# Second RMSNorm of a decoder layer: scaling the first block between the last residual additions

## The chip, the cores and the metric

One core of a Trainium2 chip runs the whole layer in one launch. The metric is device microseconds from the start to the end of one execution; the figure for a kernel is the median of three executions. PE is the matrix engine, PEld its weight loads, DVE the vector engine, ACT the scalar engine, POOL the GpSimd engine, SP the queue that issues the transfers.

## The reference, cut to what matters

Every tensor is float32. Only the lines around the second norm matter here; 1088 tokens (1024 of the prompt and 8 x 8 of the samples) with 1024 channels pass through them.

```python
x = x + jnp.concatenate([a, o], axis=-1) @ w_out           # output projection, residual
h = rms_norm(x, norm_ffn_g)                                # x * rsqrt(mean(x*x) + EPS) * g, per token
g_full = jnp.concatenate([ffn_past, h @ w_ffn_gate], axis=1)
g = depthwise_conv_valid(g_full, ffn_conv_w, ffn_conv_b)   # causal, width 3
x = x + (jax.nn.silu(g) * (h @ w_ffn_up)) @ w_ffn_down     # w_ffn_gate, w_ffn_up: 1024 x 2816
```

## The kernel before

Channels lie on the 128 partitions and tokens along the free axis, so x is eight tiles `x2[0..7]` of 128 x 1088. Each float32 product is made from two rounded parts per operand, `hi` and `lo`, as three matmuls: hi x hi, hi x lo and lo x hi. `split` (L907) makes them: ACT copies `hi` (L909), DVE subtracts to get `lo` (L910). The tokens fall into two halves of HN = 544 columns.

**Last part of the output projection.** `out_half(h, hook)` (L974) walks over the eight tiles m. For each it forms one product (`block_product`, 2 chunks x 2 k x 3 = 12 matmuls of 272 columns, L849 to L852) in one of four PSUM pairs; DVE adds it to x (L982), SP stores x to DRAM (L983), ACT squares it (L985), and from m = 1 on DVE adds the square to a running sum (L989). The half h = 0 comes first, then h = 1. A hook is called after each m of the second half.

**The norm.** `root` (L185) sums over the partitions with five matmuls against a column of ones, which run as ten (L192, in one PSUM pair), and makes the reciprocal root of each token on DVE and ACT (L196 to L207). `spread` (L210) turns that column back into a row on all partitions with five transposes on PE (L219) and two ACT copies (L221). Its result `rs[0]` serves the first half, `rs[1]` the second. `scale` (L993, L995) multiplies a tile by the norm's weight and that row, in place, on DVE.

**The first gate and up products.** `first_blocks(k, tag)` scales and splits four tiles of the first half. `first_half` (L1019) multiplies them with two weight blocks at once (`two_products`, L855): per tile k there are 12 matmuls, 6 into `px` and 6 into `py`. Four tiles are `b11`, the other four `b21`; between the two, ACT copies the partial results out of PSUM (L1026). The same products follow for the up weights (`up0`), and `second_half` for the other half of the tokens. The remaining ten pairs of blocks of the gated network (`ffn_pair`, L1111) run by a Strassen-like scheme of seven products, whose sums and differences of weights start with the addition at L952.

**What sets the order.** Each engine works through its own queue in order and stops at an instruction whose inputs are not there. The queues are laid out when the kernel is built, by a planner that goes by program order and by its own estimates of when things are ready. `tc.issue_after(ins)` pins the instructions traced inside it behind `ins` in the queue of the engine of `ins`; it adds no wait between engines. In the kernel before, the scales of the first block stand behind `added`, the last running sum of the second half, and so do the splits:

```python
def first_blocks(k, tag, after):
    for i in range(k, k + 4):
        with tc.issue_after(made[-2] if len(made) > 1 else after):
            scale(0, i, rs[0])
        with tc.issue_after(after):
            split(x2[i][:, :HN], tag, i - k)
```

`made` lists the DVE subtractions of the splits in the order in which they were traced; `made[7]` is that of the eighth tile.

Of the kernel before, what the change touches and what calls it, by code (L numbers as in the profile page):

```python
# [5 lines left out]

# [1 line left out]

# [54 lines left out]
HN = N // 2  # L65
HF = NF // 2
PO = 240
# [10 lines left out]
def trunk_kernel(tc, xT, w_in, w_out, w_gate, w_up, w_down, par, kc, vc, sa, sf, pmask, smask,  # L78
                 yT, kT, vT, ca, cas, cf):
    nc = tc.nc  # L80
    with (
# [34 lines left out]
        def zt(z, tag, bufs, s, w=N, dt=F32):  # L116
            return zone[z].tile([P, w], dt, tag=tag, name=nm(s), bufs=bufs)

        def keep(s, w=N):
            return tp.tile([P, GW], F32, tag="T", name=nm(s))[:, :w]  # L120
# [64 lines left out]
        def root(sq, div, width):  # L185


            ps = bank(*rbank[0])
            size = sizes(width)
            nt = len(size)  # L190
            for i, n in enumerate(size):
                nc.tensor.matmul(ps[:n, i:i + 1], sq[:, i * P:i * P + n], ones, start=True, stop=True)  # L192
            v = sp.tile([P, 9], F32, tag="rv", name=nm("rv"), bufs=2)[:, :nt]
            nc.vector.memset(v, 1.0)
            nf = width // P
            nc.vector.tensor_scalar(v[:, 0:nf], ps[:, 0:nf], 1.0 / div, EPS, op0=ALU.mult, op1=ALU.add)  # L196
            if nf < nt:
                n = size[-1]
                nc.vector.tensor_scalar(v[:n, nf:nt], ps[:n, nf:nt], 1.0 / div, EPS, op0=ALU.mult, op1=ALU.add)
            r = sp.tile([P, 9], F32, tag="rr", name=nm("rr"), bufs=2)[:, :nt]  # L200
            nc.vector.reciprocal(r, v)
            nc.scalar.activation(r, r, AF.Sqrt)

            t = sp.tile([P, 9], F32, tag="rt", name=nm("rt"), bufs=2)[:, :nt]
            nc.vector.tensor_mul(t, r, r)
            nc.vector.scalar_tensor_tensor(t, t, -0.5, v, op0=ALU.mult, op1=ALU.mult)
            nc.vector.scalar_tensor_tensor(r, t, 1.5, r, op0=ALU.add, op1=ALU.mult)  # L207
            return r
# [55 lines left out]
        with ExitStack() as order:  # L264
            for k in range(KT):
                t = keep("x")
# [488 lines left out]
        i = 0  # L755
        for p in range(NS1, NP):
            prompt_heads(i, HEADS[p - NS1])
            i = HEADS[p - NS1]
# [12 lines left out]
        x2 = []  # L771
# [42 lines left out]
        for p, upto in zip(range(NS1, NP), SHEADS):  # L814
            prompt_heads(i, upto)
            i = max(i, upto)
# [13 lines left out]
        def pair(s="g"):  # L830

            return zone["Fps"].tile([P, 1024], F32, tag="g2", name=nm(s), bufs=4)
# [4 lines left out]
        def slot(tag, s, dt=F32R, w=HN):  # L837
            return zt("F", tag, 8, s, HN, dt)[:, :w]

        def block_product(o, w, x, start):  # L840

            whi, wlo = w
            nk = len(x)
            for c in range(2):
                n = HN // 2
                ps = o[:, PO:512] if c == 0 else o[:, 512:PO + HN]
                for k, (xh, xl) in enumerate(x):
                    t = slice(c * n, c * n + n)
                    nc.tensor.matmul(ps, whi[:, k, :], xh[:, t], start=(start and k == 0), stop=False,  # L849
                                     skip_group_check=True)  # L850
                    nc.tensor.matmul(ps, whi[:, k, :], xl[:, t], start=False, stop=False, skip_group_check=True)  # L851
                    nc.tensor.matmul(ps, wlo[:, k, :], xh[:, t], start=False, stop=(k == nk - 1),  # L852
                                     skip_group_check=True)

        def two_products(outs, ws, x, start, hook=lambda k, last: None):  # L855


            n = HN // 2
            nk = len(x)
            for k, (xh, xl) in enumerate(x):  # L860
                for o, (whi, wlo) in zip(outs, ws):
                    for c in range(2):
                        ps = o[:, PO:512] if c == 0 else o[:, 512:PO + HN]
                        t = slice(c * n, c * n + n)
                        nc.tensor.matmul(ps, whi[:, k, :], xh[:, t], start=(start and k == 0), stop=False,
                                         skip_group_check=True)
                        nc.tensor.matmul(ps, whi[:, k, :], xl[:, t], start=False, stop=False, skip_group_check=True)
                        last = nc.tensor.matmul(ps, wlo[:, k, :], xh[:, t], start=False, stop=(k == nk - 1),
                                                skip_group_check=True).ins
                hook(k, last)  # L870

        def all_of(ps):
            return ps[:, PO:PO + HN]

        def halves(x):
            return x[:, :HN], x[:, HN:N]
# [3 lines left out]
        n = PARTS[-1]  # L880
# [24 lines left out]
        made = []  # L905

        def split(x, tag, k):  # L907
            hi, lo = slot(tag, tag + "h"), slot(tag, tag + "l")
            nc.scalar.activation(hi, x, AF.Copy)  # L909
            made.append(nc.vector.tensor_sub(lo, x, hi.bitcast(F32)).ins)  # L910
            blocks[tag][k] = hi, lo
# [6 lines left out]
        def weight_raw(w, j):  # L918
            raw = []
            for i in (j, j + HF):  # L920
                raw.append(wp.tile([P, D], F32, tag="WR", name=nm("wr"), bufs=WR))
                with tc.issue_after(last_load):
                    nc.sync.dma_start(raw[-1], w[i])
            return raw
# [9 lines left out]
        def block_tile(x, zone=False):  # L934

            t = zt("F", "WA", 2, "wa", D, F32R) if zone else wp.tile([P, D], F32R, tag="W", name=nm("wb"))
            hi, lo = t[:, :half], t[:, half:]
            nc.scalar.activation(hi, x, AF.Copy)  # L938
            nc.gpsimd.tensor_sub(lo, x, hi.bitcast(F32))  # L939
            return [t.rearrange("p (k c) -> p k c", c=P) for t in (hi, lo)]  # L940
# [4 lines left out]
        def weight_blocks(w, j):  # L945

            g, u = weight_raw(w, j)
            g1, g2, u1, u2 = g[:, :half], g[:, half:], u[:, :half], u[:, half:]
            a11 = block_tile(g1, True)
            a12 = block_tile(g2, True)  # L950
            x = zt("F", "tmp", 4, "s1", HN)[:, :half]
            nc.vector.tensor_add(x, u1, u2)  # L952
            nc.vector.tensor_sub(u1, g1, u1)
            nc.vector.tensor_sub(g1, x, g1)  # L954
            s2 = block_tile(g1)
            s1 = block_tile(x)
            nc.vector.tensor_sub(g2, g2, g1)
            s3 = block_tile(u1)
            s4 = block_tile(g2)
            a22 = block_tile(u2)  # L960
            return [a11, a12, a22, s1, s2, s3, s4]
# [12 lines left out]
        def out_half(h, hook):  # L974


            c = slice(h * HN, h * HN + HN)
            for m in range(KT):
                ps = pair()
                block_product(ps, wl[m], part[h], True)  # L980
                x = x2[m][:, c]
                added = nc.vector.tensor_add(x, all_of(ps), x).ins  # L982
                nc.sync.dma_start(x2d[m][:, c], x)  # L983
                s = slot("t1", "sq", F32)
                nc.scalar.activation(s, x, AF.Square)  # L985
                if m == 0:
                    acc = s
                else:
                    added = nc.vector.tensor_add(acc, s, acc).ins  # L989
                hook(m, added)  # L990
            return acc, added

        def scale(h, k, r):  # L993
            x = x2[k][:, h * HN:h * HN + HN]
            nc.vector.scalar_tensor_tensor(x, x, col(C_GFFN + k), r, op0=ALU.mult, op1=ALU.mult)  # L995

        def new_root(s):
            return slot("t3", s, F32)

        sq0, _ = out_half(0, lambda *_: None)  # L1000
        rs = []

        def norm_first(m, added):
            if m == 1:
                rs.append(root(sq0, D, HN))
            elif m == 4:
                rs[0] = spread(rs[0], new_root, HN)

        def first_blocks(k, tag, after):
            for i in range(k, k + 4):  # L1010
                with tc.issue_after(made[-2] if len(made) > 1 else after):
                    scale(0, i, rs[0])
                with tc.issue_after(after):
                    split(x2[i][:, :HN], tag, i - k)

        sq1, added = out_half(1, norm_first)
        quads = [(*halves(x2[k]), *halves(x2[k + 4])) for k in range(4)]

        def first_half(w, between=lambda: None, hook=lambda k, last: None):  # L1019
# [20 lines left out]

        def between():
            rs.append(root(sq1, D, HN))
            first_blocks(4, "b21", added)

        def spread_second(k, last):
            if k == 1:
                with tc.issue_after(last):
                    rs[1] = spread(rs[1], new_root, HN)

        first_blocks(0, "b11", added)  # L1050
        g1, g_shared = first_half(gate0, between, spread_second)
        r1 = rs[1]
        for k in range(4):
# [2 lines left out]
        u1, u_shared = first_half(up0)  # L1056
# [54 lines left out]
        def ffn_pair(j):  # L1111
# [58 lines left out]
            if j:  # L1170
                products(weight_blocks(w_up, j), u11, put_u)
                return
# [215 lines left out]
```

## Time and profile before

| | |
|---|---|
| median of three runs | 1409.12 us |
| the three runs | 1405.84 to 1413.22 us |
| the profiled execution, its own time | 1410.36 us |
| its span, first to last instruction | 1408.6 us |
| PE busy in the span | 1348.9 us, 96% |
| DVE, ACT, POOL busy | 844.7, 521.9, 447.0 us |
| mean granted PE clock | 0.982 |

The span is that of the profiled execution alone; 1.8 us of its own time lie outside it. The output projection's last part and the first blocks of the second norm lie between 600 and 657 us. A busy share is an average over the whole span, so it tells little of these 57 us; the rows below are taken from them.

### The profile page before, as it was taken

The numbers are of one execution on the slowest core, as the hardware profiler recorded it, in microseconds if no ns is written. First come the engines' busy times: TensorE is split into PE (matmuls) and PEld (weight loads), VectorE is DVE, ScalarE is ACT, GpSimd is POOL, SyncE is SP. The second block draws the span as 40 slices with busy tenths as digits, with TensorE's granted clock in tenths as the row PEclk, the third lists the DMA queues.
The fourth block names the chain that finished last, engine by engine and source line by source line (L and its number), as shares of the span: only waits on it lengthen the run. The fifth ranks groups of instructions, "written<-read, shape, count | busy, mean of one in ns | idle before, by whom it ended". The sixth has DMA issues, their size and how long they took to land.

```text
span 1408.6 us, 25028 instructions
## 1 busy us (share of the span) xinstructions
PE 1348.9 (96%) x10059; PEld 1282.0 (91%) x10059; DVE 844.7 (60%) x1636; ACT 521.9 (37%) x1047; POOL 447.0 (32%) x362
## 2 busy tenths in 40 slices
PE   6999999999998999988999999999999999999995
PEld 6988879899977777988999999999999999999995
DVE  7398595556674656677965555665655543322146
ACT  5312212456564564254533333333332332112033
POOL 3221111111001103330754654554654222233124
PEclk9999999999999999998999999999999999999998
DMA  7247676836798878450112222212222672313003
GB/s 275 57 140 248 222 256 206 224 111 168 197 266 229 256 213 257 128 195 24 47 50 89 93 77 77 92 47 77 92 78 77 202 275 60 117 57 123 12 16 113
DMA packets 84884, 195.17 MB, mean 139 GB/s; under 512 B 12576, under 2 KB 46752, under 8 KB 84768
## 3 DMA queue, kind: packets, MB, share of 16 engines
q1 hardware_dynamic: 84768, 193.57, 43.7%
q8 instruction: 79, 1.29, 0.4%
q14 instruction: 37, 0.30, 0.1%
HBM read 145.03 MB, written 48.52 MB: 137 GB/s over the span
## 4 chain that ended last, share of the span: by engine, by line
PE 76%; DVE 10%; issue 5%; DMA 5%; POOL 2%; ACT 1%; SPq 1%; POOLq 0%; DVEq 0%; ACTq 0%
PE g L174 10%; PE g L172 10%; PE g L173 10%; PE py L849 4%; PE py L851 4%; PE py L852 4%; DVE cacc L342 4%; PE o L675 3%; PE s L590 3%; PE pz L852 3%; PE pz L849 3%; PE pz L851 3%; PE px L849 3%; PE px L852 3%; PE px L851 3%
## 5 line engine op out<-in xcount | busy, mean ns | idle before, releaser
L148 POOL TENSOR_TENSOR wl<-wr,wh 128x768 fp32r<-128x768 f32 (+2 forms) x61 | 116.8, 1916 | 461.6 <-PE g L174 373.6
L172 PE MATMUL g<-xh,wh 128*128 128x384 f32 (+1 forms) x472 | 158.1, 335 | 0.0
L173 PE MATMUL g<-xl,wh 128*128 128x384 f32 (+1 forms) x472 | 156.6, 332 | 0.0
L174 PE MATMUL g<-xh,wl 128*128 128x384 f32 (+1 forms) x472 | 156.5, 332 | 0.0
L173 PE MATMUL g<-al,wh 128*128 128x384 f32 (+1 forms) x432 | 143.2, 332 | 1.7 <-DVE al L1203 1.7
L172 PE MATMUL g<-ah,wh 128*128 128x384 f32 (+1 forms) x432 | 141.6, 333 | 2.2 <-ACT ah L1202 0.8
L174 PE MATMUL g<-ah,wl 128*128 128x384 f32 (+1 forms) x432 | 142.7, 332 | 0.7 <-POOL wl L148 0.7
L146 ACT ACTIVATE wh<-wr 128x768 fp32r<-128x768 f32 (+2 forms) x62 | 52.0, 839 | 240.1 <-PE g L174 177.8
L939 POOL TENSOR_TENSOR wb<-wr,wb 128x512 fp32r<-128x512 f32 x84 | 115.2, 1383 | 56.8 <-ACT wb L938 56.8
L1225 DVE TENSOR_TENSOR x<-g,x 128x384 f32<-128x384 f32 (+1 forms) x72 | 38.0, 534 | 137.8 <-PE g L174 137.6
L938 ACT ACTIVATE wb<-wr 128x512 fp32r<-128x512 f32 x84 | 52.4, 628 | 164.2 <-DVE wr L954 105.0
L631 ACT ACTIVATE y<-y,m 128x128 f32<-128x128 f32 (+1 forms) x192 | 88.4, 463 | 32.2 <-DVE m L619 32.1
L1143 DVE SCALAR_TENSOR_TENSOR fc<-gb,prm,fc 128x1104 f32<-128x1104 f32 x44 | 83.5, 1918 | 14.7 <-ACT fc L1141 14.4
L174 PEld LDWEIGHTS g<-xh,wl 128*128 128x128 f32 x472 | 89.3, 189 | 2.6 <-issue 2.5
L172 PEld LDWEIGHTS g<-xh,wh 128*128 128x128 f32 x472 | 89.6, 190 | 1.4 <-issue 1.2
L173 PEld LDWEIGHTS g<-xl,wh 128*128 128x128 f32 x472 | 89.6, 190 | 1.1 <-issue 1.0
L594 DVE CUSTOM_DVE_ANT_0 y<-s,pmk 128x128 f32<-128x128 f32 (+1 forms) x192 | 63.9, 378 | 41.6 <-PE s L590 33.2
L939 POOL TENSOR_TENSOR wa<-wr,wa 128x512 fp32r<-128x512 f32 x42 | 54.9, 1308 | 101.0 <-ACT wa L938 101.0
L172 PEld LDWEIGHTS g<-ah,wh 128*128 128x128 f32 x432 | 81.7, 190 | 3.1 <-ACT ah L1202 1.1
L173 PEld LDWEIGHTS g<-al,wh 128*128 128x128 f32 x432 | 82.1, 190 | 2.4 <-DVE al L1203 2.4
L174 PEld LDWEIGHTS g<-ah,wl 128*128 128x128 f32 x432 | 82.1, 190 | 1.0 <-POOL wl L148 1.0
L342 DVE SCALAR_TENSOR_TENSOR cacc<-gp,prm,cacc 128x1024 f32<-128x1024 f32 x60 | 77.9, 1299 | 0.1
(358 smaller groups left out, 4133.0 us busy)
## 6 DMA issues: line engine op xcount, KB each, us to landing
cr<-in_kc SPq DMA_DIRECT2D x24, 768.0 KB, 8.4
cr<-in_vc SPq DMA_DIRECT2D x24, 768.0 KB, 7.1
kk<-dk SPq DMA_DIRECT2D x48, 256.0 KB, 7.5
u<-u SPq DMA_DIRECT2D x22, 544.0 KB, 3.2
ur<-u SPq DMA_DIRECT2D x22, 544.0 KB, 5.4
wr<-in_w_in SPq DMA_DIRECT2D x22, 512.0 KB, 5.2
wr<-in_w_gate SPq DMA_DIRECT2D x22, 512.0 KB, 3.3
wr<-in_w_up SPq DMA_DIRECT2D x22, 512.0 KB, 5.0
```

The lines of the kernel that those rows point to most:

```text
L148: lo_eng.tensor_sub(lo, raw, hi.bitcast(F32))
L172: nc.tensor.matmul(ps[c], whi[:, k, :], xh[:, t0:t0 + n], start=(k == 0), stop=False)
L173: nc.tensor.matmul(ps[c], whi[:, k, :], xl[:, t0:t0 + n], start=False, stop=False)
L174: nc.tensor.matmul(ps[c], wlo[:, k, :], xh[:, t0:t0 + n], start=False, stop=(k == nk - 1))
L342: eng.scalar_tensor_tensor(acc[:, :S], gp[:, j:j + S], col(w0 + j), acc[:, :S], op0=ALU.mult, op1=ALU.add)
L594: nc.vector.tensor_tensor_reduce(out=y[:, o:o + n], in0=ps[:, o:o + n], in1=mask, op0=ALU.add, op1=ALU.min, scale=1.0, scalar=3e38, accum_ ...
L631: nc.scalar.activation(y, y, AF.Exp, bias=m[:, 4 * g + i:4 * g + i + 1], scale=-1.0, accum_out=den[:, g, 2 * hd + u, i:i + 1])
L849: nc.tensor.matmul(ps, whi[:, k, :], xh[:, t], start=(start and k == 0), stop=False, skip_group_check=True)
L851: nc.tensor.matmul(ps, whi[:, k, :], xl[:, t], start=False, stop=False, skip_group_check=True)
L852: nc.tensor.matmul(ps, wlo[:, k, :], xh[:, t], start=False, stop=(k == nk - 1), skip_group_check=True)
L939: nc.gpsimd.tensor_sub(lo, x, hi.bitcast(F32))
L1143: nc.vector.scalar_tensor_tensor(c[:, :W], gb[i][:, t:t + W], col(C_FW + 3 * f + t), c[:, :W], op0=ALU.mult, op1=ALU.add)
```

## The change

The sums of squares keep their arithmetic, and so does everything else; only places and orders change.

1. `root` of the first half moves from m = 1 to m = 3 of the second half's loop, and its `spread` from m = 4 to m = 6.
2. `out_half` returns the list of residual additions. The first scale is pinned behind the addition of m = 6, the second behind that of m = 7; the others stay two splits behind. The splits are no longer pinned, so sums of squares may come later than scales.
3. In `two_products` the matmuls of tile k are pinned behind the last matmul of tile k-1 on PE, for all four calls of it.
4. The first addition of each later set of weight sums (L952) is pinned behind the eighth split of the first block.

```diff
@@ two_products
+            last = None
             for k, (xh, xl) in enumerate(x):
-                for o, (whi, wlo) in zip(outs, ws):
-                    for c in range(2):
+                with tc.issue_after(last) if last else nullcontext():
+                    for o, (whi, wlo) in zip(outs, ws):
+                        for c in range(2):
...
-                        last = nc.tensor.matmul(ps, wlo[:, k, :], xh[:, t], start=False, stop=(k == nk - 1),
-                                                skip_group_check=True).ins
+                            end = nc.tensor.matmul(ps, wlo[:, k, :], xh[:, t], start=False, stop=(k == nk - 1),
+                                                   skip_group_check=True).ins
+                last = end
                 hook(k, last)
@@ weight_blocks
-            nc.vector.tensor_add(x, u1, u2)
+            with tc.issue_after(made[7]):
+                nc.vector.tensor_add(x, u1, u2)
@@ out_half
+            residuals = []
...
-                added = nc.vector.tensor_add(x, all_of(ps), x).ins
+                residuals.append(nc.vector.tensor_add(x, all_of(ps), x).ins)
...
-                    added = nc.vector.tensor_add(acc, s, acc).ins
-                hook(m, added)
-            return acc, added
+                    nc.vector.tensor_add(acc, s, acc)
+                hook(m)
+            return acc, residuals
@@ norm_first
-            if m == 1:
+            if m == 3:
                 rs.append(root(sq0, D, HN))
-            elif m == 4:
+            elif m == 6:
                 rs[0] = spread(rs[0], new_root, HN)
@@ first_blocks
-                with tc.issue_after(made[-2] if len(made) > 1 else after):
+                with tc.issue_after(made[-2] if len(made) > 1 else residuals[6 + i]):
                     scale(0, i, rs[0])
-                with tc.issue_after(after):
-                    split(x2[i][:, :HN], tag, i - k)
+                split(x2[i][:, :HN], tag, i - k)
```

## Rows read from the trace of the kernel before

**Rows 1.** By stretch: us, busy PE PEld DVE ACT POOL, granted clock, DMA, GB/s.
```profile
618.80:622.40 3.60, 0.00 (x0) 0.02 (x1) 3.46 (x5) 2.47 (x5) 1.03 (x2) 1.00 0.57 190
623.30:626.60 3.30, 3.30 (x17) 3.27 (x17) 1.86 (x8) 0.91 (x2) 1.81 (x2) 0.52 0.47 168
...
635.10:638.80 3.70, 0.01 (x1) 0.01 (x1) 3.50 (x6) 1.34 (x3) 0.00 (x0) 0.77 0.40 151
637.50:647.30 9.80, 8.51 (x39) 8.48 (x40) 9.77 (x19) 4.87 (x9) 0.00 (x0) 0.50 0.01 3
...
656.80:1360.00 703.20, 697.73 (x5114) 695.73 (x5113) 373.89 (x461) 221.90 (x305) 301.12 (x261) 1.00 0.26 87
```

**Rows 2.** PE's longest waits from 600 to 700 us: in total, times, longest.
```profile
PE px L865 <- DVE x L995: 3.7, 1, 3.7
PE g L192 <- DVE sq L989: 3.7, 1, 3.7
```

**Rows 3.** Timeline of PE: start, duration, work, idle before and its releaser.
```profile
612.21 0.29 PE L849 MATMUL g<-mh,wh 128*128 128x272 f32 x1
...
613.71 0.29 PE L849 MATMUL g<-mh,wh 128*128 128x272 f32 x1
...
618.47 0.29 PE L852 MATMUL g<-mh,wl 128*128 128x272 f32 x1
622.41 1.20 PE L192 MATMUL g<-ones,sq 128*128 128x1 f32 x10 [3.65 <-DVE sq L989]
623.54 0.59 PE L849 MATMUL g<-mh,wh 128*128 128x272 f32 x1
...
624.38 0.43 PE L849 MATMUL g<-mh,wh 128*128 128x272 f32 x1
624.61 0.43 PE L851 MATMUL g<-ml,wh 128*128 128x272 f32 x1
...
629.60 0.77 PE L219 MATMUL g<-ident,rr 128*128 128x128 f32 x5
...
634.80 0.28 PE L852 MATMUL g<-mh,wl 128*128 128x272 f32 x1
638.79 0.60 PE L865 MATMUL px<-b11h,wa 128*128 128x272 f32 x1 [3.71 <-DVE x L995]
...
639.41 1.89 PE L192 MATMUL g<-ones,sq 128*128 128x1 f32 x10
641.23 0.59 PE L867 MATMUL px<-b11l,wa 128*128 128x272 f32 x1
...
656.84 0.29 PE L865 MATMUL px<-b11h,wa 128*128 128x272 f32 x1
```

**Rows 4.** Timeline of DVE, in the same columns.
```profile
621.55 0.71 DVE L989 TENSOR_TENSOR sq<-sq,sq 128x544 f32<-128x544 f32 x1
622.73 1.24 DVE L989 TENSOR_TENSOR sq<-sq,sq 128x544 f32<-128x544 f32 x1 [0.47 <-ACT sq L985]
...
635.12 0.72 DVE L982 TENSOR_TENSOR x<-g,x 128x544 f32<-128x544 f32 x1 [0.15 <-PE g L852]
...
636.62 0.73 DVE L989 TENSOR_TENSOR sq<-sq,sq 128x544 f32<-128x544 f32 x1
637.27 1.48 DVE L995 SCALAR_TENSOR_TENSOR x<-x,prm,rb 128x544 f32<-128x544 f32 x2
638.77 0.73 DVE L910 TENSOR_TENSOR b11l<-x,b11h 128x544 fp32r<-128x544 f32 x1
...
655.90 5.66 DVE L995 SCALAR_TENSOR_TENSOR x<-x,prm,rb 128x544 f32<-128x544 f32 x8 [7.27 <-ACT rb L221]
```

**Rows 5.** Timeline of ACT: copies of the spread row, first copies of the split.
```profile
630.24 0.69 ACT L221 ACTIVATE rb<-g 128x512 f32<-128x512 f32 x2 [0.46 <-PE g L219]
...
638.08 1.35 ACT L909 ACTIVATE b11h<-x 128x544 fp32r<-128x544 f32 x2 [1.49 <-DVE x L995]
```

**Rows 6.** Timeline of POOL beside the sums of squares.
```profile
621.71 3.40 POOL L939 TENSOR_TENSOR wb<-wr,wb 128x512 fp32r<-128x512 f32 x2 [2.56 <-ACT wb L938]
```

More of the change, by code (lines that the diff above doesn't have):

```diff
@@ L9 @@
-from contextlib import ExitStack, contextmanager
+from contextlib import ExitStack, contextmanager, nullcontext
 import numpy as np
@@ L859, in two_products @@
             nk = len(x)
+            last = None
             for k, (xh, xl) in enumerate(x):
-                for o, (whi, wlo) in zip(outs, ws):
-                    for c in range(2):
[L863 to L867, printed above, removed]
-                        last = nc.tensor.matmul(ps, wlo[:, k, :], xh[:, t], start=False, stop=(k == nk - 1),
-                                                skip_group_check=True).ins
+                with tc.issue_after(last) if last else nullcontext():
+                    for o, (whi, wlo) in zip(outs, ws):
+                        for c in range(2):
+                            ps = o[:, PO:512] if c == 0 else o[:, 512:PO + HN]
+                            t = slice(c * n, c * n + n)
+                            nc.tensor.matmul(ps, whi[:, k, :], xh[:, t], start=(start and k == 0), stop=False,
+                                             skip_group_check=True)
+                            nc.tensor.matmul(ps, whi[:, k, :], xl[:, t], start=False, stop=False,
+                                             skip_group_check=True)
+                            end = nc.tensor.matmul(ps, wlo[:, k, :], xh[:, t], start=False, stop=(k == nk - 1),
+                                                   skip_group_check=True).ins
+                last = end
                 hook(k, last)
@@ L998, in new_root, with norm_first, first_blocks @@
             return slot("t3", s, F32)
-        sq0, _ = out_half(0, lambda *_: None)
+        sq0, _ = out_half(0, lambda m: None)
         rs = []
-        def norm_first(m, added):
-            if m == 1:
+        def norm_first(m):
+            if m == 3:
                 rs.append(root(sq0, D, HN))
-            elif m == 4:
+            elif m == 6:
                 rs[0] = spread(rs[0], new_root, HN)
-        def first_blocks(k, tag, after):
+        def first_blocks(k, tag):
             for i in range(k, k + 4):
-                with tc.issue_after(made[-2] if len(made) > 1 else after):
+                with tc.issue_after(made[-2] if len(made) > 1 else residuals[6 + i]):
                     scale(0, i, rs[0])
-                with tc.issue_after(after):
-                    split(x2[i][:, :HN], tag, i - k)
-        sq1, added = out_half(1, norm_first)
+                split(x2[i][:, :HN], tag, i - k)
+        sq1, residuals = out_half(1, norm_first)
         quads = [(*halves(x2[k]), *halves(x2[k + 4])) for k in range(4)]
@@ L1042, in between @@
             rs.append(root(sq1, D, HN))
-            first_blocks(4, "b21", added)
+            first_blocks(4, "b21")
         def spread_second(k, last):
@@ L1048, in spread_second @@
                     rs[1] = spread(rs[1], new_root, HN)
-        first_blocks(0, "b11", added)
+        first_blocks(0, "b11")
         g1, g_shared = first_half(gate0, between, spread_second)
```

## The prediction

> **What bounds the kernel now.** I read the busy time by stretch first. From 656.8 to 1360 us PE works 697.73 of 703.20 us at full clock [rows 1], so what PE gains before 656.8 us should reach the end, and work hidden under PE there costs nothing. Ahead of it lie two stretches in which PE does next to nothing: 618.8 to 622.4 and 635.1 to 638.8 us. The list of waits names one wait in each, 3.7 us long: the matmuls of `root` wait for a running sum, and the first product of the norm waits, through the split, for the first scale [rows 2]. They are the two longest waits of PE between 600 and 700 us.
>
> The timeline of PE places them [rows 3]. The first half's products are over and two of the second are done at 618.76 (618.47 + 0.29). `root` is next in the queue and stands until 622.41, though the product of m = 2 behind it does not need it. The last product of the projection ends at 635.08, and the first of the norm starts at 638.79. In between DVE does the last addition, two sums of squares, then the first scale at 637.27 [rows 4], then ACT the first `hi` at 638.08 [rows 5].
>
> Each wait has a second price, the clock. A product's twelve matmuls take 1.50 us at full clock (612.21 to 613.71) [rows 3], 0.126 us each. After the first wait matmuls start 0.227 us apart (624.38 to 624.61) [rows 3], and the stretch from 623.3 to 626.6 shows a granted clock of 0.52; that from 637.5 to 647.3 shows 0.50 [rows 1]. So of the two levels, 2.4 and 1.2 GHz, the lower one stood for about 3.1 us of PE's work after the first wait and for 8.3 us after the second (638.79 to about 647.1), with 1.3 us of idle time ahead of that.
>
> What these cost: first wait 3.65 us, its clock 3.1 x (1 - 0.126/0.227) = 1.4 us. Second wait 3.71 us; its clock: the matmuls in 638.79 to 639.41 and 641.23 to 647.07 make 6.46 us x 0.445 = 2.9, and `root` of the second half took 1.82 us (639.41 to 641.23) where it took 1.13 at 622.41 [rows 3], 0.7 more, together 3.6 us. In all 12.4 us; no rearrangement of these waits can give more.
>
> **The change, part by part.** *Root at m = 3, spread at m = 6.* Nothing is added; two products pass in front of `root`. They end at 618.76 + 2 x 1.50 = 621.8. The sum that `root` waits for is ready at 622.26 (621.55 + 0.71) [rows 4], so 0.6 us of the wait is left and 3.0 us are saved. Below that I see 2.4, if DVE now takes the additions of these two products (0.65 us a step, as from 636.62 to 637.27 [rows 4]) ahead of that sum. Above it stands 3.0 + 1.4 if the clock does not fall: PE would do next to nothing for 0.6 + 1.13 us rather than 3.65 + 1.13, and after that much I think it likelier to hold than not. I take 3.7. `spread` at m = 6 must not come late for the scale. Its matmuls at 629.60 gave a row at 630.93 (630.24 + 0.69) [rows 3, 5], 1.33 us later. With one product behind it in the queue, 0.70 + 1.50 us from its start to the end of PE's last product E, the row is there at E - 0.9. It is hidden, barely; a further product behind would have been of no use. If DVE's root arithmetic comes late for it, PE stands there instead.
>
> *Scales ahead of sums.* The first scale needs only the spread row and the addition of m = 6. From its start to PE took 1.52 us (637.27 to 638.79), ACT's copy included [rows 3 to 5]. If it starts at E - 0.9, PE starts at E + 0.6 instead of E + 3.71. DVE then has the last addition (E + 0.05 to 0.7), the first `lo` (to 1.4), the second scale, one sum of squares and the second `lo` (to about 3.4), by 0.64 to 0.74 us each [rows 4]. PE needs the `lo` after four of a tile's twelve matmuls, so it stands some 0.3 us for the first, 0.3 and 0.2 us around the second; from the third tile a tile costs DVE 0.74 + 0.64 = 1.4 us and PE 1.50, and PE is the slower. Waits 1.4 us in all, 2.3 saved; the ends are 3.1 (only the first 0.6 left) and 0 (the planner leaves the order as it is).
>
> *Clock after the second wait.* Of 3.6 us, all come back if the clock holds, 0.8 if it stays low for two stretches of 3.1 us (2 x 1.4 lost). Four short waits in some 4 us are less idle than 3.71 us at once, but not nothing; I count 1.2 lost and 2.4 back.
>
> *Matmuls of tile k behind tile k-1.* Nothing is added; PE's queue loses the freedom to use the `hi` of the next tile while a `lo` is late, which the 0.3 us above hold. It also ends `px` and `py` nearly together where before all of `px` could go first; the copies from PSUM then come later, 0 to 1.5 us per call if the next product needs their pair at once. As four PSUM pairs exist and the spread's two come free, I count 0.
>
> *Sums of squares later, pinned additions.* The same count of instructions. POOL works from 621.71 to 625.11 [rows 6], and a sum of squares under it took 1.24 us rather than 0.71 [rows 4]. Those of m = 1 and 2 still lie there, while PE no longer stands: I count 0.4 us of DVE's delay as reaching PE, between 0 and 1.0 (two such sums). The Trainium skill, page "SBUF — State Buffer", section "SBUF: two separate sides", says that DVE with two SBUF inputs and GpSimd hold the shared ports by an exclusive lock, so the loser waits out a whole instruction; by that each of the two sums could lose 1.7 us and the gain would be 3 us smaller. The trace's 1.24 us is milder than that. The pin at L952 is behind a split that ends near 648 us before; nothing here shows this addition waiting for it: 0.
>
> *Behind it.* DVE stood 7.27 us until 655.90 for the second spread row [rows 4], whose place in PE's queue moves with PE. The second half's scales therefore move with it, and PE's cover from 656.8 us on holds.
>
> Sum: 3.7 + 2.3 + 2.4 - 0.4 = 8.0 us. Against the profiled execution's 1410.36 us that is 1402.4; this execution lies 1.24 us above the median of the runs, 1409.12, so by the median 1401.1 us.
>
> **The rivals.** *The clock stays low (same).* PE starts earlier, but waits a few tenths at every tile and stays at 1.2 GHz as long as before. For it: at 638.79 to 647.1 PE was fully busy and still at 0.50 [rows 1]. Against it: at half clock a tile takes PE 2.7 us and DVE 1.4, so the waits end at once. Gain 3.0 + 2.3 - 0.4 = 4.9, time 1404.2. The Trainium skill, page "TensorE: Matmul & The Clock Gate", section "A second HAM failure mode: psum-queue depth-cycling", tells of just this: many micro-idles between groups, and the clock swings between its levels. The trace bears it out so far as idling of 3.7 us goes.
>
> *The order on DVE does not come out (same).* The pins only forbid; a planner that finds sums of squares ready keeps putting them ahead of the scales, and only the first wait goes. Gain 2.5 to 4.5, time 1405.6. For it: DVE was busy 3.50 of the 3.70 us of the second wait [rows 1]. Against it: with the row there 0.9 us before E, the first scale has nothing to wait for while the last product runs.
>
> *The second root stalls PE (slower).* Scales and splits may now stand ahead of the last sum of squares, and `root` of the second half waits for it in PE's queue in front of the products, as it stood third there at 639.41 [rows 3]. It is harmless while the sum comes within a microsecond. Each further microsecond costs one; from about 8 the gain is gone. At the worst, all eight scales and splits first, 8 x 1.4 = 11 us after E, PE then does nearly all eight tiles at 1.50 us after E + 12 + 1.1, with low clock for 3 us or all of it: E = 632.1 puts the end of the blocks at 660 to 665 instead of 656.8, time 1412 to 1418.
>
> **How the numbers follow.** Forecast 0.64, own range 1398.5 to 1403.5 (sum between 5.6 and 10.6); clock 0.13; order 0.15; second root 0.08. Faster by over 0.5% means a gain over 7.0 us, about what this kernel's measurement can tell from no change: 0.52, four fifths of the forecast's chance. The same: 0.12 of the forecast, 0.13 for the clock, 0.15 for the order and 0.02 of the third rival, 0.42. Slower by over 0.5%: 0.06. The range leaves out the third rival and gains over 12.4 us: 1396.7 to 1408.0, whose upper end is a gain of 1.1 us.
>
> **What would show it.** Right: PE's wait for the running sum at `root` falls to about 0.6 us, PE idle from the last product of the projection to the first of the norm to about 0.6 us, the granted clock between the two stays near 1, the first product of `up0` starts near 649 us instead of 656.84. Wrong: `root` of the second half waiting on a sum, a scale behind both last sums on DVE, a granted clock of 0.5 for 8 us, or new waits of PE behind 650 us, for PSUM pairs above all.

## The result, and the profile after

The changed kernel takes 1400.91 us, the median of ten runs (1398.08 to 1405.29); the kernel before, ten runs beside it, 1410.11 us (1400.99 to 1420.02). The ratio is 0.9947, with a 95% interval of 0.9927 to 0.9967: 7.5 us faster, between 4.7 and 10.3 (the two medians by themselves lie 9.2 apart, which is within that). The prediction said 1401.1 us and a gain of 8.0.

The profiled execution took 1401.15 us, 9.2 less than the one of before. To see where this lies I cut both at the same two places: the first residual addition of the projection's last part on DVE (606.74 us before, 604.52 after) and the first product of the up weights on PE (656.84 before [rows 3], 647.09 after). Up to the first cut 2.2 us differ, in a part that the change does not touch. Between the cuts it is 50.10 against 42.57 us, 7.5 less. Behind the second cut it is 751.8 against 752.3 us. So in these two profiles the gain is made in this stretch. That the part behind it is 0.5 us longer means little: two profiles of one program differ there by 0.3 to 0.9 us (table below).

The stretch in both kernels, from the busy time by stretch (us, then busy time with instructions of PE, PEld, DVE, ACT and POOL, then granted clock, DMA share, GB/s), first before, then after with three parts of it:

```profile
606.74:656.84 50.10, 42.74 (x295) 41.67 (x293) 38.37 (x64) 24.34 (x42) 12.56 (x8) 0.86 0.37 132
```

```profile
604.52:647.09 42.57, 39.25 (x295) 37.93 (x294) 36.63 (x62) 24.02 (x42) 12.62 (x8) 0.96 0.45 155
619.50:631.30 11.80, 8.69 (x66) 8.04 (x65) 11.73 (x24) 8.20 (x14) 3.42 (x2) 1.00 0.77 253
631.40:634.70 3.30, 3.29 (x15) 3.29 (x15) 3.30 (x6) 1.32 (x3) 0.00 (x0) 0.50 0.07 24
634.80:647.00 12.20, 12.11 (x95) 11.65 (x95) 6.42 (x16) 4.90 (x10) 0.00 (x0) 1.00 0.01 2
```

PE stands 3.3 us in the stretch where it stood 7.4. The low clock is left in one place, 3.4 us long, where it stood for over 3 and some 10 us before [rows 1]. The waits themselves, in the list of PE's waits after (in total, times, longest) and in PE's timeline (start, duration, work, idle before and its releaser):

```profile
PE px L869 <- DVE b11l L914: 1.4, 1, 1.4
PE px L867 <- ACT b11h L913: 1.1, 1, 1.1
...
PE g L192 <- DVE sq L995: 0.7, 1, 0.7
```

```profile
619.22 0.29 PE L852 MATMUL g<-mh,wl 128*128 128x272 f32 x1
...
620.22 1.18 PE L192 MATMUL g<-ones,sq 128*128 128x1 f32 x10 [0.71 <-DVE sq L995]
625.93 0.77 PE L219 MATMUL g<-ident,rr 128*128 128x128 f32 x5
...
628.10 0.29 PE L852 MATMUL g<-mh,wl 128*128 128x272 f32 x1
629.50 0.39 PE L867 MATMUL px<-b11h,wa 128*128 128x272 f32 x1 [1.12 <-ACT b11h L913]
629.73 0.28 PE L867 MATMUL py<-b11h,wb 128*128 128x272 f32 x1
631.41 0.60 PE L869 MATMUL px<-b11l,wa 128*128 128x272 f32 x1 [1.40 <-DVE b11l L914]
...
634.30 1.29 PE L192 MATMUL g<-ones,sq 128*128 128x1 f32 x10
...
645.78 0.77 PE L219 MATMUL g<-ident,rr 128*128 128x128 f32 x5
```

The wait of 3.65 us at `root` [rows 3] has become 0.71. The 3.71 us between the projection and the norm [rows 3] have become 1.12 for the first `hi` and 1.40 for the first `lo`. Why these two are longer than the 0.6 and 0.3 us of the prediction stands in the timelines of DVE and ACT:

```profile
627.35 0.72 DVE L995 TENSOR_TENSOR sq<-sq,sq 128x544 f32<-128x544 f32 x1
627.99 0.78 DVE L1001 SCALAR_TENSOR_TENSOR x<-x,prm,rb 128x544 f32<-128x544 f32 x1
628.68 0.72 DVE L995 TENSOR_TENSOR sq<-sq,sq 128x544 f32<-128x544 f32 x1
629.32 0.71 DVE L988 TENSOR_TENSOR x<-g,x 128x544 f32<-128x544 f32 x1
629.95 0.77 DVE L1001 SCALAR_TENSOR_TENSOR x<-x,prm,rb 128x544 f32<-128x544 f32 x1
630.64 0.71 DVE L914 TENSOR_TENSOR b11l<-x,b11h 128x544 fp32r<-128x544 f32 x1
```

```profile
626.83 0.66 ACT L221 ACTIVATE rb<-g 128x512 f32<-128x512 f32 x2
...
628.79 0.66 ACT L913 ACTIVATE b11h<-x 128x544 fp32r<-128x544 f32 x1 [0.61 <-DVE x L1001]
```

The spread row is there at 627.49 (626.83 + 0.66), 0.9 us before the last product ends at 628.39 (628.10 + 0.29), as predicted. But DVE is still adding a sum of squares, so the first scale starts 0.5 us later, at 627.99. A second sum stands between that scale and the last addition, and the second scale between it and the first `lo`, which is done at 631.35 instead of 629.8: 0.9 us of this are the sums, 0.7 the second scale. PE in turn has only two matmuls to do with the first `hi` before it needs the `lo` (629.50 and 629.73).

### The profile page after: what moved, and what is told of

The parts are those of the page before. It is cut to its first block, busy times and chain, and to the rows that moved or that the text cites. A ratio compares the mean times of both kernels' runs of the same rounds, so it can differ in the third digit from the quotient of the medians.

```text
span 1399.4 us, 25027 instructions
## 1 busy us (share of the span) xinstructions
PE 1344.4 (96%) x10059; PEld 1277.8 (91%) x10059; DVE 842.3 (60%) x1636; ACT 521.7 (37%) x1047; POOL 444.1 (32%) x362
## 4 chain that ended last, share of the span: by engine, by line
PE 79%; DVE 10%; DMA 5%; issue 2%; ACT 1%; SPq 1%; POOL 1%; POOLq 0%; DVEq 0%; ACTq 0%
PE g L174 9%; PE g L172 9%; PE g L173 9%; PE py L851 4%; PE py L849 4%; PE py L852 4%; DVE cacc L342 4%; PE o L675 3%; PE s L590 3%; PE pz L849 3%; PE px L849 3%; PE pz L852 3%; PE px L852 3%; PE px L851 3%; PE pz L851 3%; PE t L658 3%
## 5 line engine op out<-in xcount | busy, mean ns | idle before, releaser
L943 POOL TENSOR_TENSOR wa<-wr,wa 128x512 fp32r<-128x512 f32 x42 | 62.1, 1482 | 144.7 <-ACT wa L942 139.6
```

## The experiments

All are read by the same stretch, first residual addition to first product of the up weights. The table comes from the busy time by stretch of each run; low clock is twice the stretch times one less the mean granted clock, rounded as that clock is, so good to half a microsecond. "First" is PE's wait at `root` of the first half, "hi" and "lo" those for the first rounded tile of the norm (a dash where there is none). "Behind" is the time from the end of the stretch to the end of the span.

| run | stretch us | PE idle | granted clock | low clock us | first, hi, lo | behind us |
|---|---|---|---|---|---|---|
| before | 50.10 | 7.36 | 0.86 | 14.0 | 3.65, 3.71, - | 751.8 |
| before again | 50.50 | 7.29 | 0.86 | 14.1 | 3.58, 3.71, - | 751.4 |
| after | 42.57 | 3.32 | 0.96 | 3.4 | 0.71, 1.12, 1.40 | 752.3 |
| root moved alone | 44.79 | 4.81 | 0.92 | 7.2 | 0.59, 4.13, - | 749.7 |
| scales alone | 47.14 | 7.62 | 0.96 | 3.8 | 3.71, 0.69, 2.03 | 749.9 |
| waits filled | 44.94 | 1.39 | 1.00 | 0 | 0.59, 0.70, - | 753.8 |
| waits filled, timed | 46.69 | 1.62 | 0.96 | 3.7 | 0.82, 0.71, - | 752.9 |
| no pins on PE | 42.53 | 3.20 | 0.96 | 3.4 | 0.62, 1.11, 1.40 | 751.1 |
| root at m = 2 | 46.40 | 4.12 | 0.89 | 10.2 | 2.09, 0.54, 1.40 | 751.7 |
| late sums | 41.06 | 2.82 | 1.00 | 0 | 0.57, 0.67, 0.96 | 754.0 |
| late sums, timed | 41.58 | 2.37 | 0.96 | 3.3 | 0.66, 0.66, 0.97 | 753.7 |
| late sums, early spread | 42.28 | 3.12 | 1.00 | 0 | 0.69, 0, 0.42 | 753.8 |
| POOL later | 43.51 | 2.68 | 0.92 | 7.0 | 0.69, 0.52, 1.40 | 750.9 |
| late sums, POOL later | 41.57 | 2.39 | 0.96 | 3.3 | 0.67, 0.43, 1.20 | 751.8 |

**The kernel before, again.**

> The kernel before, run again, to see how well one profile repeats. The measure in all these runs is the stretch from the first residual addition of the last projection part to the first product of the up weights: 50.10 us before (606.74 to 656.84), 42.57 us after (604.52 to 647.09). Every theory expects 50.1 us within 0.3, with the two waits of 3.65 and 3.71 us and the low clock behind each in their places; if it differs by over 1 us, differences of that size between the other runs mean nothing.

Measured: 50.50 us, waits of 3.58 and 3.71 us. The waits repeat to 0.1 us and the stretch to 0.4, a little more than the 0.3 expected. The low clock does not repeat in its places: it stood for some 7 us behind either wait, where the first profile had over 3 and some 10. So waits can be compared to a tenth, stretches only with their low clock beside them. The parts ahead of the stretch differ by 5.6 us between these two profiles of one program, which is why whole times of single runs are not used here.

**Root and spread moved alone.**

> Only the places of root (m = 3) and spread (m = 6) change; scales, splits and pins are as before. Theory that the two waits are two separate costs: the wait at root falls to 0.7 us and the clock stays full there, 4.4 us saved as in the changed kernel; the second wait stays at 3.7 us with its low clock; stretch 45.6 us. Rival, that DVE is the bound of this stretch and the time only moves from one wait to the other: the second wait grows by most of it; stretch 48 to 50 us.

```diff
-            if m == 1:
+            if m == 3:
                 rs.append(root(sq0, D, HN))
-            elif m == 4:
+            elif m == 6:
                 rs[0] = spread(rs[0], new_root, HN)
```

```profile
624.88 1.18 PE L192 MATMUL g<-ones,sq 128*128 128x1 f32 x10 [0.59 <-DVE sq L989]
...
637.19 0.60 PE L865 MATMUL px<-b11h,wa 128*128 128x272 f32 x1 [4.13 <-ACT b11h L909]
```

Measured: 44.79 us. The first wait falls to 0.59 us with the clock held; the second grows by only 0.4. The rival, in which the time only moves to the second wait, falls. The stretch is 0.8 us shorter than expected because the low clock behind the second wait stood for some 7 us here and not for 10.

**Scales alone.**

> All of the change but the places of root (m = 1) and spread (m = 4), which are as before. Theory of separate costs: the first wait stays 3.65 us with low clock behind it; scales between the last additions save what the changed kernel saved behind its last product, 3.0 us; stretch 47.1 us, a little less if the earlier spread lets the first scale go sooner. Rival, that the scales gain only because root was moved: stretch 49.5 us or more.

Edit: the changed kernel with `m == 1` and `m == 4` put back in `norm_first`.

```profile
617.79 1.22 PE L192 MATMUL g<-ones,sq 128*128 128x1 f32 x10 [3.71 <-DVE sq L995]
...
631.13 0.39 PE L867 MATMUL px<-b11h,wa 128*128 128x272 f32 x1 [0.69 <-ACT b11h L913]
633.67 0.40 PE L869 MATMUL px<-b11l,wa 128*128 128x272 f32 x1 [2.03 <-DVE b11l L914]
...
641.81 0.39 PE L867 MATMUL px<-b21h,wa 128*128 128x272 f32 x1 [0.97 <-ACT ta L1031]
```

Measured: 47.14 us, as the theory had it. The first wait stays whole; behind the last product PE stands 0.69 and 2.03 us. Here the clock held behind these two waits (all of the 3.8 us of low clock lie behind `root`), and a further wait of 0.97 us came up between the two blocks, for ACT's copy out of PSUM. Against the mean of the two profiles of before, 50.30 us, the parts alone save 5.5 and 3.2 us, together 8.7; both at once save 7.7. They are two costs, nearly additive; the difference is no larger than what the clock's place moves. Each part was profiled once and neither was timed.

**The waits filled with work.**

> The kernel before, with two products into an unread PSUM pair ahead of root of the first half and two behind the last product of the projection, 3.0 us of work each, where PE stood 3.65 and 3.71 us. No order of other work changes. It prices the clock apart from the idle time. Theory that the lower clock comes from PE's idling: it stays at full in both places, the waits end when they did before, stretch 50.1 - 1.4 - 3.6 = 45.1 us. Rival, that the clock falls for another reason, or that only the idle time itself was paid for: stretch 49.5 to 50.5 us.

```diff
             if m == 1:
+                for _ in range(2):
+                    block_product(pair("fill"), wl[1], part[1], True)
                 rs.append(root(sq0, D, HN))
...
         sq1, added = out_half(1, norm_first)
+        for _ in range(2):
+            block_product(pair("fill"), wl[7], part[1], True)
```

The kernel computes all that it did; the four added products are read by nothing.

```profile
608.94:653.88 44.94, 43.55 (x342) 42.44 (x341) 38.12 (x64) 23.84 (x42) 12.51 (x8) 1.00 0.43 151
```

Measured: 44.94 us, though PE does four products more. The clock stands at 1.00 throughout, and the waits end when they did: 0.59 and 0.70 us of them are left beside the 3.0 us of filling. That is the clock's share by itself, 5.2 us of the 12.4. Timed in rounds:

> The kernel before with the filled waits, timed in rounds. In one profile the stretch took 44.94 us, 5.2 less than before, with the clock at full in it, though PE does 6 us more work. Theory that what this stretch gains reaches the end: ratio 0.9963. Rival, that a gain here is given back behind 656 us: 0.999 to 1.001.

The profile of this run shows 46.69 us, with low clock from some 638.6 us on for over 3 us, though PE had worked without a pause since 636.23, after a wait of 0.71 us. The ratio is 0.9987 (0.9969 to 1.0005), 1.8 us, from 4.4 faster to 0.7 slower. The expected 0.9963 lies outside; the second profile's 3.6 us (46.69 against 50.30, the mean of the two profiles of before) lie inside. How much of the clock's share a run gets back thus varies from one to the next. Some of it is lost again behind the stretch: this part took 753.8 and 752.9 us in the two profiles, and 751.8 and 751.4 in those of the kernel before; through what, the runs leave open. The rival's 0.999 to 1.001 is not excluded either, as the interval reaches 1.0005.

**No pins on PE.**

> The changed kernel without the pins of tile k behind tile k-1 on PE; DVE's, ACT's and POOL's queues stay instruction for instruction the same, PE's differs in the order of the norm's products. Theory that these pins cost and bring nothing: the same waits at root (0.7 us), first hi (1.1) and first lo (1.4); stretch 42.6 us within 0.3. Rival, that the pins carry a part of the gain by keeping px and py from running apart: stretch 43.5 us or more, with a new wait of PE between 636 and 647 us. Rival, that they cost: below 42 us.

```diff
-                with tc.issue_after(last) if last else nullcontext():
+                with nullcontext():
```

Measured: 42.53 us, each wait within 0.1 us of those of the changed kernel. The pins on PE are worth nothing here, in either direction. The pin at L952 changes nothing at all: without it the queues of all engines are instruction for instruction the same.

**Root one product earlier.**

> The changed kernel with root of the first half one product earlier, at m = 2. PE has 1.5 us less work before it, so it stands some 2.2 us for the running sum instead of 0.71; nothing else is touched. Theory that only long idling brings the clock down: if 2.2 us are still held, the stretch is 42.6 + 1.5 = 44.1 us or, as DVE catches up meanwhile, 43.6; if the clock falls, 1.4 more, 45 to 45.5 us. Rival, that DVE sets the time of the stretch and a wait moved on PE costs nothing: 42.6 us.

```diff
-            if m == 3:
+            if m == 2:
                 rs.append(root(sq0, D, HN))
```

```profile
602.89:649.29 46.40, 42.28 (x294) 40.96 (x293) 37.35 (x62) 23.95 (x42) 12.51 (x8) 0.89 0.41 145
619.30:622.80 3.50, 3.50 (x18) 3.47 (x19) 2.62 (x6) 1.92 (x3) 1.90 (x2) 0.51 0.81 276
633.00:639.40 6.40, 6.40 (x32) 6.37 (x31) 6.31 (x13) 2.49 (x5) 0.00 (x0) 0.50 0.01 3
```

Measured: 46.40 us. PE stands 2.09 us at `root`, and the clock falls behind it (0.51 from 619.3 to 622.8); it did not behind 0.57 to 0.82 us in ten profiles. DVE catches up meanwhile, so the wait for the first `hi` is 0.54 us. The low clock behind it lasted 6.4 us this time, which puts the stretch 0.9 us above the expectation. The two products that the change puts in front of `root` are worth the clock besides their own 3.0 us.

**Sums of squares later.**

> The changed kernel with the sums of squares of m = 4 to 7 put behind the second lo on DVE. In the changed kernel one such sum ran ahead of the first scale, one between it and the last addition. Theory that these sums are what made PE's two waits 1.1 and 1.4 us where the prediction had 0.6 and 0.3: the waits shrink to 0.6 and about 1.0 us (the second scale still ahead of the first lo); stretch 41.7 us, 40.3 if the clock holds. Rival, that the sums are not in the way and only the spread row counts: waits as before, 42.6 us. Rival, that the late sums now stop root or spread of the second half: a new wait of 1 us or more there, 43 us or more.

```diff
-                else:
+                elif h == 0 or m < 4:
                     nc.vector.tensor_add(acc, s, acc)
+                else:
+                    late.append(s)
...
         first_blocks(0, "b11")
+        for s in late:
+            with tc.issue_after(made[1]):
+                nc.vector.tensor_add(sq1, s, sq1)
```

DVE's timeline in this run:

```profile
630.20 0.79 DVE L1003 SCALAR_TENSOR_TENSOR x<-x,prm,rb 128x544 f32<-128x544 f32 x1 [0.69 <-ACT rb L221]
631.09 0.72 DVE L988 TENSOR_TENSOR x<-g,x 128x544 f32<-128x544 f32 x1
631.74 0.78 DVE L1003 SCALAR_TENSOR_TENSOR x<-x,prm,rb 128x544 f32<-128x544 f32 x1
632.43 0.72 DVE L914 TENSOR_TENSOR b11l<-x,b11h 128x544 fp32r<-128x544 f32 x1
```

Measured: 41.06 us, waits of 0.67 and 0.96 us. The first scale now waits for the spread row (0.69 us) and no longer for sums; 0.67 us is the predicted 0.6. What is left of the `lo` wait is the second scale in front of it. So the sums were what lengthened PE's two waits, by 0.9 us together. Timed:

> The run with late sums, timed in rounds. Its stretch took 41.06 us in one profile, 1.5 less than the changed kernel's 42.57 and 9.0 less than before. Theory: ratio to the kernel before 0.9936. Rival, that a new wait behind the stretch (PE stood 1.1 us for a weight part from POOL there) takes it back: 0.995 or more.

The ratio is 0.9957 (0.9938 to 0.9976), not the expected 0.9936. The stretch took 41.58 us in this profile, the clock having fallen for 3.3 us, and behind it PE stands 1.1 us for a weight part from POOL (0.5 us for ACT in the changed kernel as well); the part behind the stretch takes 753.7 us where the changed kernel took 752.3. The rival's figure, 0.995 or more, holds.

**Sums later and spread earlier.**

> As the run with late sums, but the sums of m = 2 to 7 are late, the first spread stands behind m = 5 and the first scale behind the addition of m = 5. Theory: the first two scales and the first lo are done by the end of the last product, so both waits of PE there vanish and the clock holds: 42.6 - 2.5 - 1.4 = 38.7 us, to which come up to 1 us at the first spread and up to 1.5 at the second, whose roots now come late; 39 to 41 us. Rival, that DVE has too much in front of the blocks whatever the order, so PE stands as long in all: 42 us or more.

Edit: as in the run with late sums, but `m < 2`, spread at `m == 5` and the scales' pins at `residuals[5 + i]`.

```profile
630.67 0.78 DVE L1003 SCALAR_TENSOR_TENSOR x<-x,prm,rb 128x544 f32<-128x544 f32 x1
631.37 0.72 DVE L1061 TENSOR_TENSOR sq<-sq,sq 128x544 f32<-128x544 f32 x1
632.00 0.72 DVE L914 TENSOR_TENSOR b11l<-x,b11h 128x544 fp32r<-128x544 f32 x1
632.64 0.78 DVE L1003 SCALAR_TENSOR_TENSOR x<-x,prm,rb 128x544 f32<-128x544 f32 x1
```

Measured: 42.28 us; the expected 39 to 41 us fall. PE begins the norm without a wait and the clock holds at 1.00, but now a tile costs DVE 1.97 us (630.67 to 632.64: scale, sum, `lo`), more than PE's 1.50, and PE waits a little at each, besides 0.85 us at the spread. The rival is right: with sums between the tiles DVE sets the pace.

**POOL later, and both.**

> The changed kernel, but the second pair of first up blocks is rounded behind the eighth hi on ACT, so that POOL's two subtractions (619.52 to 622.94 in the changed kernel) run some 20 us later and no sum of squares runs beside them. In the changed kernel the two sums beside them took 1.16 and 1.18 us, where 0.71 is usual. Theory that this delay reaches PE through DVE's full queue, as the prediction counted with 0.4 us: the two sums take 0.7 us and PE's two waits behind the last product are shorter by 0.4 to 0.9 us together; stretch 41.7 to 42.2 us, 40.3 if the clock then holds. Rival, that DVE makes it up before the first scale: waits as before, 42.6 us. The raw weights stand longer in their buffer, so a later load may come late: a new wait of PE behind 650 us would show it.

```diff
-        up0 += [block_tile(raw[1][:, i * half:i * half + half]) for i in range(2)]
...
         g1, g_shared = first_half(gate0, between, spread_second)
+        with tc.issue_after(his[7]):
+            up0 += [block_tile(raw[1][:, i * half:i * half + half]) for i in range(2)]
```

`his` lists ACT's copies of the splits.

```profile
634.41 0.39 PE L867 MATMUL px<-b11h,wa 128*128 128x272 f32 x1 [0.52 <-ACT b11h L913]
636.32 0.40 PE L869 MATMUL px<-b11l,wa 128*128 128x272 f32 x1 [1.40 <-DVE b11l L914]
```

Measured: the two sums take 0.71 us each, and the wait for the first `hi` falls from 1.12 to 0.52 us; the one for the first `lo` stays. POOL's neighbourhood cost PE 0.6 us. The stretch is nonetheless 43.51 us, as the low clock stood for 7 us here; by the stretch alone the expectation fails, by the waits it holds.

How long a sum takes beside POOL follows from where it starts. In the changed kernel, DVE and POOL:

```profile
608.32 1.81 DVE L995 TENSOR_TENSOR sq<-sq,sq 128x544 f32<-128x544 f32 x1
...
620.63 1.16 DVE L995 TENSOR_TENSOR sq<-sq,sq 128x544 f32<-128x544 f32 x1
621.71 0.71 DVE L988 TENSOR_TENSOR x<-g,x 128x544 f32<-128x544 f32 x1
622.35 1.18 DVE L995 TENSOR_TENSOR sq<-sq,sq 128x544 f32<-128x544 f32 x1
```

```profile
606.54 3.01 POOL L943 TENSOR_TENSOR wa<-wr,wa 128x512 fp32r<-128x512 f32 x2 [17.28 <-ACT wa L942]
...
619.52 3.42 POOL L943 TENSOR_TENSOR wb<-wr,wb 128x512 fp32r<-128x512 f32 x2 [2.57 <-PE g L852]
```

The sum at 622.35 starts 0.59 us before POOL's second subtraction of that pair ends (622.94, 619.52 + 3.42) and takes 0.47 us more than 0.71. The sum at 608.32 starts 1.23 us before the end of the other pair (609.55) and takes 1.10 us more. In the fourteen profiles, all 88 sums that start while a subtraction of POOL runs are longer by what is left of it, less 0.11 to 0.14 us. The addition at 621.71, which reads one input from PSUM, takes 0.71 us beside POOL.

> Late sums (m = 4 to 7 behind the second lo) and POOL's two subtractions later, together. Theory of separate small costs: stretch 40 to 41 us, whole time below the changed kernel's by 1.5 to 2.5 us, ratio to the kernel before 0.992 to 0.994. Rival, that DVE's sums only move from one wait to another: 41 to 42.5 us and a ratio as that of the changed kernel, 0.995.

Measured: 41.57 us with 3.3 us of low clock, ratio 0.9940 (0.9915 to 0.9964). The two waits behind the last product are 0.43 and 1.20 us, 1.63 together as with late sums alone, so the two remedies do not add. The stretch fits the rival, the ratio the theory, and the interval holds the changed kernel's 0.9947 too. None of the later versions is told apart from the changed kernel by its time.

## Why the prediction was right

The mechanism held but for one step, the order of work on DVE. The two sizes that were furthest off, the first two below, nearly cancelled, so it is luck that the total came within half a microsecond.

1. *Root and spread, 3.7 us.* Measured 4.5: from the first addition to the end of the last product it is 28.34 us before (606.74 to 635.08) and 23.87 after (604.52 to 628.39). The predicted 0.6 us of wait is 0.71, the clock holds (1.00 from 619.5 to 631.3), so the upper bound of 4.4 was the better choice. Alone and at m = 2 the runs show why: 0.6 us held the clock, 2.1 us did not.
2. *Scales ahead of sums, 2.3 us.* Measured 1.2: waits of 2.52 us (1.12 + 1.40) instead of 3.71, where 1.4 was predicted. This is the term that was mis-sized. The step that failed is the one that let the first scale start with the spread row and DVE go straight on to the addition and the first `lo`; the sums in front of both were not counted. Put late, they gave 0.67 and 0.96. The second scale, too, stands in front of the first `lo` (0.69 us in that run, 631.74 to 632.43), where the prediction had it behind; the kernel before shows this order already, both scales in one row and then the `lo` [rows 4]. And PE needs the `lo` after two matmuls (629.50 and 629.73) and not after four. Of the 1.12, POOL accounts for 0.6 by the run with POOL later, where the sum had 0.4 as a term of its own. The Trainium skill, page "SBUF — State Buffer", section "SBUF: two separate sides", has the loser of the shared ports blocked while the other's instruction runs. The traces agree: a sum waits for the rest of POOL's subtraction, 0.45 and 0.47 us here. The prediction's 1.7 us for each sum took the whole subtraction instead of its rest; the 1.24 us that it called milder fits the rest as well.
3. *Clock after the second wait, 2.4 us.* Measured 2.2: 3.6 us were lost before, 1.4 after. The matmuls from 631.41 to 634.30 take 2.9 us x 0.445 = 1.3, `root` 1.22 us (634.30 to 635.52) instead of 1.13. In other profiles of like waits the low clock stood for nothing or for over 6 us, so this agreement is partly luck.
4. *Pins, 0.* Right for PE's by a run without them; L952's changes no queue.
5. *The second root.* It stands at 634.30 with no wait of PE's before it, and the second spread at 645.78 without one: the rival that would have made the kernel slower did not come about. Sums late by four tiles did not bring it either.
6. *Behind the stretch.* PE's cover held in the main. Of 7.5 us, 0.5 are missing at the end, with one new wait of PE for a weight part (0.5 us), but this part varies by itself: one wait of PE for ACT's `ah` (L1202 before, L1207 after), some 470 us behind the stretch, took 0.78 and 2.57 us in the two profiles of the kernel before and 2.30 in the changed one.

The terms add up to 4.5 + 1.2 + 2.2 = 7.9; the stretch gains 7.5. The rest was not measured by itself. Some 0.26 us of it can be the one stop more that PE makes (an estimate: a last matmul runs 0.16 us longer than to the next one's start, 0.29 against 0.126 us, and a first one takes 0.23 us to the next, 629.50 to 629.73, 0.10 more than 0.126).

The rival of the clock stood nearer than its chance said: in the runs with 1.4 us for the first `lo`, low clock always followed, for 3.4 us in two and for 6.4 and 7.0 in two. Behind the 2.03 us of scales alone it did not, so the length of that wait does not settle it. The Trainium skill, page "TensorE: Matmul & The Clock Gate", section "A second HAM failure mode: psum-queue depth-cycling", describes such swings by short idling. These traces agree in part: 0.66 and 0.97 us of waiting lowered the clock in one profile of a program, and 0.67 and 0.96 did not in the other.

## What to carry to other kernels

An in-order engine that stops for a small reduction should first be given work from behind it; two products here were worth 3.0 us and the clock 1.4 more. When a chain is cleared, count everything that stands in the queue of the engine that feeds it, not only what the chain needs: sums that nobody was waiting for cost PE 0.9 us (2.52 us with them in front, 1.63 with them late). With the waits nearly gone the feeding engine sets the pace, and moving its work about gained nothing here that the whole time could tell.

## What the runs showed of the hardware that was not expected

The low clock is not a fixed price of a wait. One program, profiled twice, showed over 3 and some 10 us of it behind its two waits, then some 7 and 7; another none and then 3.3 us. Waits of 0.57 to 0.82 us at `root`, with 1.2 us of one-column matmuls behind them, never brought it (ten profiles); 2.09 us and more always did (four). Behind the last product the length of a wait tells less: waits of 0.69 and 2.03 us (`hi` and `lo`) did not bring it, 0.54 and 1.40 us did, and once it came some 2.4 us after a wait of 0.71 us, while PE was at work. That idling matters at all rests on the filled waits: with work in both places the low clock stood for nothing in one profile and 3.7 us in the other, where it had stood for 14. At the low clock a matmul of 272 columns starts every 0.227 us and at the full one every 0.126, so the loss is 45% of the time and not half [rows 3]. And a sum of two SBUF tiles on DVE that starts while POOL subtracts is held up for the rest of that subtraction, less 0.11 to 0.14 us, in all 88 cases.
